# Moving each matmul's activation half to a fixed start in memory

## The chip, the cores and the metric

The kernel runs on one core of one Trainium2 chip. The core has five engines that run side by side: TensorE (PE in the profile) multiplies matrices, VectorE (DVE), ScalarE (ACT) and GpSimd (POOL) work on elements, and SyncE (SP) issues most of the DMA transfers. Operands lie in SBUF, a memory of 128 partitions; TensorE's results go to PSUM. The metric is the device time of one execution in microseconds (us); lower is better.

## What is computed

One step of a one-layer decoder trunk, in float32, for 256 tokens of a new sequence and 8 times 4 tokens of running ones: T = 288 tokens in all, of D = 2048 channels.

```python
h = rmsnorm(x, norm1_g)
proj = h @ w_in + b_in                      # 2048 -> 3072
a, gate, z = split(proj)
u = a * sigmoid(gate)
c = silu(layernorm(depthwise_causal_conv(u_ext, conv_w, conv_b), ln_g, ln_b))
d = multiscale_pool(z_ext, pos0)            # windows 2, 4, 8, 16
p = einsum("btgc,gce->btge", d, pool_w) * pool_scale
x = x + concat([c, p]) @ w_out              # 2048 -> 2048
h2 = rmsnorm(x, norm2_g)
f = square(relu(h2 @ w_ff1))                # 2048 -> 8192
x = x + f @ w_ff2                           # 8192 -> 2048
y = rmsnorm(x, norm_f)
```

The outputs are y and the new states of the convolution and of the pooling.

## The kernel before

Activations lie with channels on the partitions: a tile of 128 channels by 288 tokens. Every product is made of matmuls with a stationary 128x128 block of weights and such a tile as the moving operand, 288 columns wide, adding up in a PSUM bank.

To keep float32 accuracy with TensorE's float32r operands, each operand is split in two halves, a rounded value (hi) and the rest (lo). Activations have tiles like hh and hl (the first norm's output), ah and al (the second's), fh and fl (the squared MLP values), ph and pl, mh and ml (the mixed groups), dh and dl (the pooling). Weights are loaded as raw tiles `wr` of 128 x 4 x 256 words by SP, and split on ScalarE (line 246) and VectorE or GpSimd (line 247) into `whi` and `wlo`. A product of two blocks then takes three matmuls: hi times hi (line 253), weights hi times activation lo (254), weights lo times activation hi (255). `gemm` runs over the activation tiles and, inside, over two output tiles. The first product (lines 316 to 348) does the same in its own loop, with its matmuls on line 342: eight on hh, eight on hl, eight on hh for each pair of activation tiles.

The stages follow one another: the first product and its norm; the other columns of w_in, with the convolution (VectorE, line 395) and the pooling beside them; pool_w; w_out in two halves with the layer norm between; then four times a quarter of w_ff1 (8 groups of 96 matmuls, moving operands ah and al) and a quarter of w_ff2 (8 groups of 96, moving operands fh and fl); and the last norm.

The order of work on each engine is made when the program is built, as are the places of tiles. Pools are laid out one behind the other in the order of the code. The one named `wraw` holds six raw tiles, `wspl` four hi and four lo weight tiles of 4096 bytes a partition. `actp`, right behind it, holds 64 tiles of 288 words, 1152 bytes a partition, end to end: 40 under the tag `act`, 16 under `p`, and 8 under `c`, which hold the convolution's results and later halves of ah and al. Behind it come `tmpp` and `prdp`. A tile is given out in turn, when its last reader is done. Nearly all halves are made by `act` (lines 111 and 112); the convolution's results on line 381.

Of the kernel before, what the change touches and what calls it, by code (L numbers as in the profile page):

```python
# [9 lines left out]
F32 = mybir.dt.float32  # L10
F32R = mybir.dt.float32r
# [5 lines left out]
P = 128  # L17
# [3 lines left out]
T = SEQ + NB * NS  # L21
# [15 lines left out]
ZO = PH + SEQ  # L37
ZL = ZO + NB * ZS
LATER = 1000000


GROUPS = (3, 2, 1, 0)
# [38 lines left out]
def trunk_kernel(ctx: ExitStack, tc: tile.TileContext, io):  # L81
# [6 lines left out]
    actp = ctx.enter_context(tc.tile_pool(name="actp", bufs=40))  # L88
# [8 lines left out]
    def nm(s):  # L97
        seen[s] = seen.get(s, 0) + 1
        return f"{s}{seen[s]}"

    @contextmanager
    def later(by=LATER):

        tc.cur_priority += by
        yield
        tc.cur_priority -= by

    def row(name):
        return rowp.tile([P, T], F32, name=nm(name), tag="row")

    def act(name, **kw):
        return actp.tile([P, T], F32R, name=nm(name), **(kw or {"tag": "act"}))

    def tmp(name, n=T, tag="tmp", bufs=6):
        return tmpp.tile([P, n], F32, name=nm(name), tag=tag, bufs=bufs)
# [1 line left out]
    def ms(name, n=512):  # L117
        return msp.tile([P, n], F32, name=nm(name), tag="ms", padded_shape=[P, 512])
# [10 lines left out]
    def samples(ap, n):  # L129
        return ap.rearrange("p (b t) -> p b t", t=n)  # L130

    def windows(ap, *dims):
        return bass.AP(ap.tensor, ap.offset, [ap.ap[0], *dims])
# [8 lines left out]
    def v(key, j):  # L142
        return vec[:, OFF[key] + j : OFF[key] + j + 1]
# [175 lines left out]
    for c in range(8):  # L319
# [5 lines left out]
        for k0, k1 in steps:  # L325
            for k in range(2 * c + k0, 2 * c + k1):
                hh, hl = act("hh"), act("hl")
                nc.scalar.activation(hh, xT[:, k, :], AF.Copy, scale=v("norm1_g", k))  # L328
                nc.vector.scalar_tensor_tensor(out=hl, in0=xT[:, k, :], scalar=v("norm1_g", k), in1=f32(hh), op0=ALU.mult, op1=ALU.subtract)
                pair.append((hh, hl))  # L330
            if len(steps) == 2:
                r, h, l = [t[:, :, k0, :] for t in views]
            else:
                r, h, l = first_raw[c], hi, lo
            nc.scalar.copy(h, r)  # L335
            nc.vector.tensor_tensor(l, r, h.bitcast(F32) if len(steps) == 2 else f32(hi), op=ALU.subtract)
            for w, x in ((hi, 0), (hi, 1), (lo, 0)):
                if c == 7 and w is lo:
                    token_sum(total, rows[0])
                for k in range(k0, k1):  # L340
                    for m in range(4):
                        nc.tensor.matmul(  # L342
                            first_banks[m][:, :T], lhs(w, k, m), pair[k][x],
                            start=c == 0 and k == 0 and w is hi and x == 0, stop=c == 7 and k == 1 and w is lo,
                        )
                if c == 7 and w is hi and x == 0:
                    square(6)
                    square(7)
                    rows = [row("tot")]
                    nc.vector.tensor_tensor(rows[0], squares[:, 0, 0], squares[:, 0, 1], op=ALU.add)  # L350
# [8 lines left out]
    cs = {}  # L359
# [16 lines left out]
    def conv_taps(pair):  # L376

        with later():
            pc, cw = {}, {}
            for i in pair:  # L380
                cs[i] = actp.tile([P, T], F32, name=nm("c"), tag="c", bufs=8)
                pc[i] = cvp.tile([P, SEQ], F32, name=nm("pc"), tag="cv", padded_shape=[P, 512])
                cw[i] = vec[:, CWO + i * CW : CWO + (i + 1) * CW]
                nc.scalar.activation(pc[i], u_all[:, i, 0:SEQ], AF.Identity, bias=v("conv_b", i), scale=cw[i][:, 0:1])  # L384
            for i in pair:
                prd = prdp.tile([P, NB, NS, CW], F32, name=nm("prd"), tag="prd")
                src = windows(u_all[:, i, UO:UL], (US, NB), (1, NS), (1, CW))
                nc.gpsimd.tensor_tensor(prd, src, cw[i][:, None, None, :].to_broadcast([P, NB, NS, CW]), op=ALU.mult)
                cso = cs[i][:, SEQ:T]
                nc.vector.tensor_reduce(samples(cso, NS), prd, axis=AX.X, op=ALU.add)  # L390
                nc.scalar.activation(cso, cso, AF.Identity, bias=v("conv_b", i))
            for w in range(1, CW):
                for i in pair:
                    dst = pc[i] if w < CW - 1 else cs[i][:, 0:SEQ]
                    nc.vector.scalar_tensor_tensor(out=dst, in0=u_all[:, i, w : w + SEQ], scalar=cw[i][:, w : w + 1], in1=pc[i], op0=ALU.mult, op1=ALU.add)  # L395
            for i in pair:
                if i == 0:
                    nc.gpsimd.tensor_copy(sum_c, cs[i])
                else:
                    nc.gpsimd.tensor_tensor(sum_c, sum_c, cs[i], op=ALU.add)  # L400
# [3 lines left out]
    def pool_group(g):  # L404

        bk = bank2()
        gemm(bk, hx)
        w = WINDOWS[g]
        for m in range(2):
            i = 2 * g + m  # L410
            z = z_all[:, i, :]
            zs = samples(z[:, ZO:ZL], ZS)
            p = bk[m][:, :T]
            nc.vector.tensor_tensor(p, p, rb, op=ALU.mult)
            nc.scalar.activation(z[:, PH:ZO], p[:, 0:SEQ], AF.Identity, bias=v("b_in", 16 + i))
            nc.scalar.activation(zs[:, :, PH:ZS], samples(p[:, SEQ:T], NS), AF.Identity, bias=v("b_in", 16 + i))  # L416
            b = ms("d")[:, :T]
            s, step, n = z, 1, w
            if w > 8:
                s, step, n = tmp("s", ZL, "s", 2), 4, w // 4  # L420
                nc.vector.tensor_reduce(s[:, 3:ZL], windows(z[:, 0 : ZL - 3], (1, ZL - 3), (1, 4)), axis=AX.X, op=ALU.add)
            at = PH - step * (n - 1)
            nc.vector.tensor_reduce(b[:, 0:SEQ], windows(s[:, at:], (1, SEQ), (step, n)), axis=AX.X, op=ALU.add)
            nc.vector.tensor_reduce(samples(b[:, SEQ:T], NS), windows(s[:, ZO + at :], (ZS, NB), (1, NS), (step, n)), axis=AX.X, op=ALU.add)
            nc.vector.tensor_tensor(b[:, 0 : w - 1], b[:, 0 : w - 1], rise[:, g, 0 : w - 1], op=ALU.mult)
            nc.vector.scalar_tensor_tensor(out=b[:, 0:SEQ], in0=b[:, 0:SEQ], scalar=1.0 / w, in1=z[:, PH:ZO], op0=ALU.mult, op1=ALU.subtract)
            bs = samples(b[:, SEQ:T], NS)
            nc.vector.scalar_tensor_tensor(out=bs, in0=bs, scalar=1.0 / w, in1=zs[:, :, PH:], op0=ALU.mult, op1=ALU.subtract)
            dh, dl = act("dh", tag="p", bufs=16), act("dl", tag="p", bufs=16)
            nc.scalar.copy(dh, b)  # L430
            nc.vector.tensor_tensor(dl, b, f32(dh), op=ALU.subtract)
            dd[i] = (dh, dl)
# [3 lines left out]
    def mix_group(g, banks=bank2):  # L436

        bk = banks()
        gemm(bk, [dd[2 * g], dd[2 * g + 1]])
        for m in range(2):  # L440
            i = 2 * g + m
            mh, ml = act("ph"), act("pl")
            nc.scalar.activation(mh, bk[m][:, :T], AF.Copy, scale=v("pool_scale", i))
            nc.vector.scalar_tensor_tensor(out=ml, in0=bk[m][:, :T], scalar=v("pool_scale", i), in1=f32(mh), op0=ALU.mult, op1=ALU.subtract)
            mixp[i] = (mh, ml)
# [7 lines left out]
    conv_gates(1, first_banks[2:4])  # L453
    conv_gates(0, first_banks[0:2])
    conv_taps((0, 1))
    for kind, i in SEQUENCE:
        (conv_group if kind == "conv" else mix_group if kind == "mix" else pool_group)(i)
        if kind == "conv" and (i % 2 or i == 6):
            conv_taps((i,) if i >= 6 else (i - 1, i))
        if i == 3 and kind == "conv":  # L460
            nc.sync.dma_start(z_all[:, :, ZO:ZL], io["hist_p"])
    mix_group(1)
    mix_group(0, lambda: [ms("m") for _ in range(2)])
    with later(2 * LATER):
        nc.sync.dma_start(io["u_out"], u_all[:, :, UO - CH : UL])
# [46 lines left out]
    for g in range(8):  # L512
        bk = bank2()
        gemm(bk, mixc)
        for m in range(2):
# [3 lines left out]
            kw = {"tag": "p", "bufs": 16} if k < 8 else {"tag": "c", "bufs": 8} if k >= 12 else {}  # L519
# [122 lines left out]
```

## Time and profile before

| | us |
|---|---|
| median of 3 runs | 1097.99 (1097.48 to 1098.67) |
| the profiled execution | 1098.09 |
| its span, from the first to the last instruction | 1096.3 |
| TensorE busy | 1082.3 |
| VectorE busy | 631.0 |
| ScalarE busy | 471.8 |
| GpSimd busy | 162.8 |

Busy time counts a stretch once, however many matmuls overlap in it. A matmul's row lasts about 0.3 us from its start to the end of its results, and the next one starts well before that, so the time that a matmul costs is the step from its start to the next start; a window of the trace, divided by the matmuls that it holds, gives that step.

### The profile page before, as it was taken

The page shows a single profiled execution, that of the slowest core. Times are in us where ns is not written, and L with a number is a line of the kernel's source. Part 1 is how long each engine was busy: PE and PEld are TensorE (multiplying, and loading weights), DVE is VectorE, ACT ScalarE, POOL GpSimd, SP SyncE. Part 2 cuts the span into 40 slices and gives each one's busy share as a digit, 9 for nine tenths or more (in the row PEclk, how much of TensorE's full clock was granted, in tenths as well). Part 3 has the DMA queues.
Part 4 walks back from the last instruction along what each step waited for, and adds up shares of the span by engine and source line. Part 5 has one row for each costly group of instructions (what it writes and reads, how often), then busy time and mean ns, then how long its engine had stood idle before and what let it go on. Part 6 is the DMA issues. An engine that isn't in the chain of part 4 may idle for free.

```text
span 1096.3 us, 19737 instructions
## 1 busy us (share of the span) xinstructions
PE 1082.3 (99%) x8186; PEld 1081.0 (99%) x8186; DVE 631.0 (58%) x982; ACT 471.8 (43%) x650; POOL 162.8 (15%) x108
## 2 busy tenths in 40 slices
PE   9999999999999999999999999999999999999995
PEld 9999999999999999999999999999999999999995
DVE  7798989687554544444554444555544445554553
ACT  7544454476444433334443333444433334444441
POOL 0899878500000000000000000000000000000000
PEclk9999999999999999999999999999999999999998
DMA  9655568555555555555555555555555555555522
GB/s 335 221 184 167 173 162 236 161 165 171 158 170 161 170 168 165 168 171 160 170 170 164 167 173 162 167 172 169 161 171 162 166 172 167 162 171 164 166 94 87
DMA packets 56649, 187.04 MB, mean 171 GB/s; under 512 B 5872, under 2 KB 11504, under 8 KB 56560
## 3 DMA queue, kind: packets, MB, share of 16 engines
q1 hardware_dynamic: 56416, 185.74, 54.3%
q8 instruction: 64, 1.05, 0.4%
q14 instruction: 25, 0.20, 0.1%
q10 hardware_dynamic: 144, 0.05, 0.0%
HBM read 181.49 MB, written 4.28 MB: 169 GB/s over the span
## 4 chain that ended last, share of the span: by engine, by line
PE 98%; DVE 1%; ACT 0%; DMA 0%; SPq 0%; issue 0%; DVEq 0%
PE ac L253 32%; PE ac L254 32%; PE ac L255 31%; PE ac L342 1%; PE cv L342 1%; DMA xT<-in_xT 0%; DVE xT L582 0%; PE pr L238 0%; ACT hh L328 0%; ACT uz L312 0%; PE pf L221 0%; ACT whi L335 0%; DVEq L628 0%; PE m L253 0%; PE m L254 0%
## 5 line engine op out<-in xcount | busy, mean ns | idle before, releaser
L246 ACT CAST whi<-wr 128x1024 fp32r<-128x1024 f32 x330 | 346.6, 1051 | 583.9 <-PE ac L254 553.7
L247 DVE TENSOR_TENSOR wlo<-wr,whi 128x1024 fp32r<-128x1024 f32 x272 | 333.3, 1225 | 373.7 <-ACT whi L246 373.7
L253 PE MATMUL ac<-ah,whi 128*128 128x288 f32 x1024 | 303.2, 296 | 0.0
L253 PE MATMUL ac<-fh,whi 128*128 128x288 f32 x1024 | 303.1, 296 | 0.0
L254 PE MATMUL ac<-fl,whi 128*128 128x288 f32 x1024 | 301.7, 295 | 0.0
L254 PE MATMUL ac<-al,whi 128*128 128x288 f32 x1024 | 301.6, 295 | 0.0
L255 PE MATMUL ac<-fh,wlo 128*128 128x288 f32 x1024 | 299.8, 293 | 0.0
L255 PE MATMUL ac<-ah,wlo 128*128 128x288 f32 x1024 | 299.4, 292 | 0.0
L255 PEld LDWEIGHTS ac<-fh,wlo 128*128 128x128 f32 x1024 | 193.5, 189 | 0.0
L255 PEld LDWEIGHTS ac<-ah,wlo 128*128 128x128 f32 x1024 | 193.4, 189 | 0.0
L254 PEld LDWEIGHTS ac<-fl,whi 128*128 128x128 f32 x1024 | 193.0, 188 | 0.0
L254 PEld LDWEIGHTS ac<-al,whi 128*128 128x128 f32 x1024 | 192.6, 188 | 0.0
L253 PEld LDWEIGHTS ac<-ah,whi 128*128 128x128 f32 x1024 | 192.4, 188 | 0.0
L253 PEld LDWEIGHTS ac<-fh,whi 128*128 128x128 f32 x1024 | 192.3, 188 | 0.0
L247 POOL TENSOR_TENSOR wlo<-wr,whi 128x1024 fp32r<-128x1024 f32 x58 | 138.6, 2414 | 25.2 <-ACT whi L246 23.0
L395 DVE SCALAR_TENSOR_TENSOR pc<-uz,vec,pc 128x256 f32<-128x256 f32 x232 | 98.7, 482 | 6.8 <-ACT pc L384 4.8
L253 PE MATMUL ac<-hh,whi 128*128 128x288 f32 x320 | 93.7, 296 | 0.7 <-ACT uz L416 0.7
L254 PE MATMUL ac<-hl,whi 128*128 128x288 f32 x320 | 93.8, 297 | 0.0
L255 PE MATMUL ac<-hh,wlo 128*128 128x288 f32 x320 | 88.5, 295 | 0.0
L253 PEld LDWEIGHTS ac<-hh,whi 128*128 128x128 f32 x320 | 60.3, 188 | 1.0 <-ACT uz L416 1.0
L254 PEld LDWEIGHTS ac<-hl,whi 128*128 128x128 f32 x320 | 60.4, 189 | 0.0
L255 PEld LDWEIGHTS ac<-hh,wlo 128*128 128x128 f32 x320 | 58.5, 189 | 0.0
(153 smaller groups left out, 878.2 us busy)
## 6 DMA issues: line engine op xcount, KB each, us to landing
wr<-in_w SPq DMA_DIRECT2D x336, 512.0 KB, 3.8
out_u_out<-uz SPq DMA_DIRECT2D x1, 1208.0 KB, 9.5
xT<-in_xT SPq DMA_DIRECT2D x2, 576.0 KB, 7.9
out_yT<-xT SPq DMA_DIRECT2D x2, 576.0 KB, 2.9
uz<-in_hist_c SPq DMA_DIRECT2D x1, 1088.0 KB, 11.8
wr<-in_w SPq DMA_DIRECT2D x4, 256.0 KB, 5.1
xT<-in_xT SPq DMA_DIRECT2D x3, 288.0 KB, 5.8
out_z_out<-uz SPq DMA_DIRECT2D x1, 668.0 KB, 9.8
```

The costliest lines, as they stand in the source:

```text
L246: nc.scalar.copy(hi[:, a:b, :], raw[:, a:b, :])
L247: eng.tensor_tensor(lo[:, a:b, :], raw[:, a:b, :], hi[:, a:b, :].bitcast(F32), op=ALU.subtract)
L253: nc.tensor.matmul(b, wh, xh, start=first, stop=False)
L254: nc.tensor.matmul(b, wh, xl, start=False, stop=False)
L255: nc.tensor.matmul(b, wl, xh, start=False, stop=last)
L342: nc.tensor.matmul(first_banks[m][:, :T], lhs(w, k, m), pair[k][x], start=c == 0 and k == 0 and w is hi and x == 0, stop=c == 7 and k == 1 ...
L395: nc.vector.scalar_tensor_tensor(out=dst, in0=u_all[:, i, w : w + SEQ], scalar=cw[i][:, w : w + 1], in1=pc[i], op0=ALU.mult, op1=ALU.add)
```

## The change

Each tile of the pool becomes a slot of 320 words (1280 bytes, five times 256), and the kernel uses 288 words of it from word 23 on. All operations on the halves are the same, on a slice of the slot. The pool grows from 64 x 1152 to 64 x 1280 bytes a partition.

```diff
+SLOT, SHIFT = 320, 23
...
+    def slot(name, dtype, **kw):
+        return actp.tile([P, SLOT], dtype, name=nm(name), **kw)[:, SHIFT : SHIFT + T]
+
     def act(name, **kw):
-        return actp.tile([P, T], F32R, name=nm(name), **(kw or {"tag": "act"}))
+        return slot(name, F32R, **(kw or {"tag": "act"}))
...
-                cs[i] = actp.tile([P, T], F32, name=nm("c"), tag="c", bufs=8)
+                cs[i] = slot("c", F32, tag="c", bufs=8)
```

The first word used then lies 60 bytes past a multiple of 256 in every slot.

## The prediction

> **What bounds the kernel now.** I read the page first (busy shares, the chain that ended last), then TensorE's own waits, then the step from one matmul to the next in each stage.
>
> ```profile
> span 1096.3 us, 19737 instructions
> PE 1082.3 (99%) x8186; PEld 1081.0 (99%) x8186; DVE 631.0 (58%) x982; ACT 471.8 (43%) x650; POOL 162.8 (15%) x108
> ...
> PE 98%; DVE 1%; ACT 0%; DMA 0%; SPq 0%; issue 0%; DVEq 0%
> ```
>
> ```profile
> PE pr L238 <- DVE st L235: 1.3, 1, 1.3
> PE warm L209 <- DVE ones L195: 1.1, 1, 1.1
> PE pf L221 <- ACT q L565: 1.0, 1, 1.0
> PE ac L253 <- ACT uz L416: 0.7, 1, 0.7
> PE ac L342 <- ACT whi L335: 0.4, 1, 0.4
> ```
>
> TensorE (PE) is busy 99% of the span, the chain runs over it for 98%, and all its waits for other engines come to 4.5 us. So the time is the number of matmuls times the step between two of them. The windows by stage (stretch, length, then busy us and count of PE, PEld, DVE, ACT, POOL, then granted clock and DMA) give the step:
>
> ```profile
> 34.00:150.00 116.00, 115.26 (x866) 115.02 (x866) 107.67 (x248) 50.18 (x73) 104.81 (x48) 1.00 0.55 170
> ...
> 290.00:480.00 190.00, 190.00 (x1444) 190.00 (x1443) 91.81 (x105) 72.99 (x90) 0.00 (x0) 1.00 0.54 166
> 480.00:690.00 210.00, 210.00 (x1600) 210.00 (x1600) 101.63 (x115) 80.06 (x99) 0.00 (x0) 1.00 0.55 168
> 690.00:890.00 200.00, 200.00 (x1520) 200.00 (x1520) 96.73 (x111) 77.49 (x96) 0.00 (x0) 1.00 0.54 166
> 890.00:1080.00 190.00, 190.00 (x1448) 190.00 (x1447) 95.99 (x119) 82.74 (x120) 0.00 (x0) 1.00 0.47 147
> ```
>
> In the MLP, 790 us hold 1444 + 1600 + 1520 + 1448 = 6012 matmuls: **131.4 ns each**, at full granted clock. No other engine is near its limit there (DVE 48 to 51%, DMA 47 to 55%). The change touches no matmul's shape and no count; what it can move is this step, through the address that the moving operand is read from.
>
> **Does the step know the address?** SHIFT is 23 words, 92 bytes, and the slots then begin 60 bytes past a multiple of 256; so the pool begins at 60 - 92 = -32, which is 224 past one. Tiles of 1152 bytes (4.5 times 256) end to end therefore begin at 224 and at 96 in turn. The weight tiles lie in the pool just below, in pieces of 4096 bytes, and every stationary block is 512 bytes further on, so every weight load begins at 224. Before, then, each moving half begins either at the weights' own place modulo 256, or 128 bytes from it.
>
> In the first product (L342) hh and hl are taken in turn from an empty pool: all hh begin at 224, all hl at 96. Eight matmuls on hl follow sixteen on hh. Windows laid on such runs, for matmuls that read hl, then for those that read hh:
>
> ```profile
> 17.53:18.60 1.07, 1.07 (x8) 1.00 1.07 392
> 20.71:21.78 1.07, 1.07 (x8) 1.00 1.08 367
> ```
>
> ```profile
> 18.60:20.71 2.11, 2.11 (x16) 1.00 1.05 391
> 21.78:23.88 2.10, 2.10 (x16) 1.00 1.13 356
> ```
>
> At 96: 1.07 / 8 = 133.8 ns. At 224: 2.105 / 16 = 131.6 ns. The operation, shape and weights are the same. In the second MLP product the program's placement turns the pairs over: in its first quarter, from the fifth pair on, fh lies at 224 and fl at 96; in its second quarter fh lies at 96 and fl at 224. One window on each, 72 steps long (the count has 2 more that were still running):
>
> ```profile
> 390.22:399.74 9.52, 9.52 (x74) 1.00 0.51 165
> 592.49:601.93 9.44, 9.44 (x74) 1.00 0.55 167
> ```
>
> 132.2 ns against 131.1 ns. So four arrangements take 131.1, 131.6, 132.2 and 133.8 ns, and the address alone moves the step by up to **2.7 ns**.
>
> How many steps is that worth? The groups of line 253 (out, moving operand, weights, then the count):
>
> ```profile
> L253 PE MATMUL ac<-ah,whi 128*128 128x288 f32 x1024 | 303.2, 296 | 0.0
> L253 PE MATMUL ac<-fh,whi 128*128 128x288 f32 x1024 | 303.1, 296 | 0.0
> L253 PE MATMUL ac<-hh,whi 128*128 128x288 f32 x320 | 93.7, 296 | 0.7 <-ACT uz L416 0.7
> L253 PE MATMUL ac<-ph,whi 128*128 128x288 f32 x128 | 37.7, 296 | 0.0
> L253 PE MATMUL ac<-mh,whi 128*128 128x288 f32 x128 | 35.3, 296 | 0.0
> L342 PE MATMUL ac<-hh,whi 128*128 128x288 f32 x32 | 7.5, 315 | 0.5 <-ACT whi L335 0.4
> L253 PE MATMUL ac<-dh,whi 128*128 128x288 f32 x12 | 3.2, 295 | 0.0
> L253 PE MATMUL m<-dh,whi 128*128 128x288 f32 x4 | 1.2, 296 | 0.0
> ```
>
> Lines 254 and 255 repeat each group of 253: 3 x 2640 = 7920. Line 342 has six such groups of 32 (two targets, three terms): 192. Together **8112 matmuls** read an activation half, so each ns of the step is worth 8.1 us.
>
> Why should it? The timeline shows that the next weights are read while the present operand streams: a load begins in the same 0.01 us as a matmul.
>
> ```profile
> 599.84 0.29 PE L255 MATMUL ac<-fh,wlo 128*128 128x288 f32 x1
> 599.84 0.19 PEld L253 LDWEIGHTS ac<-fh,whi 128*128 128x128 f32 x1
> ...
> 599.97 0.30 PE L253 MATMUL ac<-fh,whi 128*128 128x288 f32 x1
> ```
>
> Two streams of reads start together, and their relative place in memory matters. I read that as the two meeting in some part of SBUF. [...]
>
> **The change, part by part.**
>
> Moving operand at 60 in every matmul. The starts of both streams were equal modulo 128 in every row of before (0 or 128 bytes apart modulo 256); now they are 60 - 224 = -164, that is 92 apart modulo 256, and modulo 64 they are 28 apart. No row shows such a pair, so I bound it. Above: the worst arrangement seen, 133.8, which is also at the start nearest to 60 (36 bytes away): +2.4 ns, +19.5 us. Below: six short matmuls with full weight loads in a row of the chain,
>
> ```profile
> 285.43 0.64 PE pr L238 x6
> ```
>
> 0.64 / 6 = 107 ns for a third of the columns (line 238 streams 96); ours cannot be under that, which allows -24 ns, or -198 us: far, and no likely end. I take one full width of the effect that the rows show, downwards: 131.4 - 2.7 = 128.7 ns. The reason for the sign is that all known arrangements have the two streams in step modulo 128, the case in which they meet most, and the change is the first to take them out of it. The size is a choice, an estimate from the spread of the rows. 8112 x 2.7 ns = **-21.9 us**.
>
> Writers of the slots. The same instructions write and read them:
>
> ```profile
> L548 ACT CAST fh<-f 128x288 fp32r<-128x288 f32 x64 | 24.2, 425 | 0.0
> L549 DVE TENSOR_TENSOR fl<-f,fh 128x288 fp32r<-128x288 f32 x64 | 26.3, 452 | 0.6 <-ACT fh L548 0.6
> L559 DVE TENSOR_TENSOR xT<-xT,ac 128x288 f32<-128x288 f32 x64 | 27.3, 455 | 26.9 <-PE ac L255 26.9
> L328 ACT ACTIVATE hh<-xT,vec 128x288 fp32r<-128x288 f32 x16 | 8.4, 530 | 2.5 <-DMA xT<-in_xT 1.7 <-DMA vec<-in_vec 0.8
> ```
>
> fl, between slots at 224 and 96, takes 452 ns and an operation of the same shape outside the pool (L559) 455, so these two engines show no care for the place. Were a start at 60 to cost them 10%, it would be 45 to 53 ns each. Cover: DVE and ACT are half idle in the MLP. On the chain only three hh lie, while TensorE waits for its first operands (start, us, what):
>
> ```profile
> 6.41 0.54 ACT hh L328
> ...
> 8.03 0.44 ACT hh L328
> ...
> 9.04 0.43 ACT hh L328
> ```
>
> I cost it at 0, between -0.1 and +1.4 us (each of the three a tenth shorter, or twice as long).
>
> Conv tiles c, pool tiles dh and dl. The same argument; DVE is the one engine near its limit, 107.67 of 116 us in the convolution stretch. If TensorE gains there and DVE doesn't, its 866 matmuls keep their time and 866 x 2.7 = 2.3 us of the gain are lost. I leave the gain in: PE has 115.26 of these 116 us and waits for DVE nowhere in it.
>
> Room. 64 slots are 128 bytes longer, 8192 bytes in all; tiles behind the pool move up by 32 times 256 and keep their phase. No instruction, DMA or wait is added, no buffer count changes, no queue is passed. When PE steps 2% faster, weights have to come 2% faster: DMA at 55% and the splits on ACT and DVE at half cover that; nothing is late next. The tail after the last matmul reads xT, which doesn't move.
>
> **Sum.** The profiled execution took 1098.1 us, 1.8 over its span; the median of the runs is 1098.0, so both stand for one another. 1098.1 - 21.9 + 0 = **1076.2 us**.
>
> **The rivals.**
>
> *The meeting goes away wholly.* Then the step loses well over one width: at two to three widths, 123 to 126 ns, 44 to 66 us, 1032 to 1054. For it: the best seen arrangement is only 2.7 below the worst, so all four may be bad ones. Against: nothing shows such a step lasting. [...]
>
> *Slower: the start's own place sets the step, and 60 behaves as its neighbour 96.* Runs with the operand at 96 alone take 133.8 ns, more than any mixture; the change makes every matmul such a run. 8112 x 2.4 = +19.5: 1117.6. For it: 36 bytes is the smallest distance to any known start. Against: mixtures in which two of three matmuls read at 96 are the fastest of all (131.1). It decides as soon as the MLP's step is above 131.7.
>
> *Slower: a start inside a unit of reading costs one unit more.* All starts before are multiples of 32; 60 is none. If the unit is 16 bytes, a half has 72 units from an aligned start and 73 from 60: 131.4 / 72 = 1.8 ns, +14.8 us, 1113. No row can show it or exclude it. Were the unit 64 bytes, 32 and 60 past it touch 19 units alike, at no cost. [...]
>
> *The change does nothing to be seen.* If only bit 7 of the address counts and mixtures average out, all-60 steps 131.4 +- 0.2 ns: 1096 to 1100.
>
> **How the numbers follow.** Forecast (1058 to 1092) 0.42; wholly gone (1032 to 1058) 0.18; neighbour 96 (1105 to 1120) 0.16; one unit more (1100 to 1115) 0.14; nothing 0.10. Faster 0.60, same 0.10, slower 0.30, with 0.2% of 1098, 2.2 us, as what a measurement can tell from no change. The range leaves out half of the wholly-gone case and the upper half of the neighbour case: 1044 to 1114. Both signs hold much of the chance; the likeliest one's own range is 1058 to 1092.
>
> **What would show it.** Right: the same 8186 matmuls; the four stretches of the MLP hold about 2% more matmuls for their length, 128.7 ns each; the runs on hh and hl in the first product, and both kinds of window in the second MLP product, become equal, since all halves now begin alike. Wrong: unequal runs (then it isn't the moving start), a step over 131.7 (a slower rival; 133.2 points to one unit more, 133.8 to the neighbour), longer L548 or L549 rows, PE waits of more than 5 us in all, or a gain only in stages that DVE leaves alone.

## The result and the profile after

| | before | after |
|---|---|---|
| median of 4 runs, us | 1097.99 | 1082.97 (1082.41 to 1083.48) |
| ratio | | 0.9863, 95% interval 0.9846 to 0.988 |
| profiled span, us | 1096.3 | 1081.2 |

The change makes the kernel 15.0 us faster, against 21.9 forecast. First the head of the page after and its chain by engine, then all of TensorE's waits:

```profile
span 1081.2 us, 19737 instructions
PE 1066.8 (99%) x8186; PEld 1065.2 (99%) x8186; DVE 630.5 (58%) x982; ACT 470.7 (44%) x650; POOL 162.6 (15%) x108
...
PE 98%; DVE 1%; ACT 0%; DMA 0%; SPq 0%; DVEq 0%; issue 0%
```

```profile
PE pr L242 <- DVE st L239: 1.3, 1, 1.3
PE warm L213 <- DVE ones L199: 1.1, 1, 1.1
PE pf L225 <- ACT q L569: 1.0, 1, 1.0
PE ac L346 <- ACT whi L339: 0.8, 1, 0.8
PE ac L257 <- ACT uz L420: 0.8, 1, 0.8
```

The same 19737 instructions, the same 8186 matmuls, the same chain. TensorE's waits are 5.0 us where they were 4.5. So nothing was moved or added, and no new wait took the place of the time that went; every matmul merely costs less. Where that happened can be read from points that both chains pass: the start of the short matmuls behind each norm, and of the last sum. Before, then after (start, us, what):

```profile
33.06 0.64 PE pr L238 x6
...
217.68 0.64 PE pr L238 x6
...
1080.36 0.43 PE pf L221 x6
```

```profile
32.42 0.64 PE pr L242 x6
...
213.09 0.64 PE pr L242 x6
...
279.80 0.64 PE pr L242 x6
1065.15 0.43 PE pf L225 x6
```

With the row at 285.43 that the prediction shows, the stretches are 33.06, 184.62, 67.75, 794.93 and 15.94 us before, and 32.42, 180.67, 66.71, 785.35 and 16.05 after. They lose 0.6, 4.0, 1.0 and 9.6 us and gain 0.1. The tail, which reads xT, is untouched; every stage that streams activation halves lost time. (Of the first 0.6, the first x tile's earlier landing is 0.5: the first hh starts at 5.95 us after, 6.41 before.)

The windows show what became of the step. In the first product, on matmuls that read hl, then hh; then two stretches of the second MLP product, in the quarters that held the two mixtures before, 72 steps each (the count again has 2 that were still running):

```profile
17.16:18.20 1.04, 1.03 (x8) 1.00 1.06 399
20.29:21.32 1.03, 1.03 (x8) 1.00 1.06 381
```

```profile
18.20:20.29 2.09, 2.08 (x16) 1.00 1.05 391
21.32:23.41 2.09, 2.08 (x16) 1.00 1.12 357
```

```profile
388.00:397.36 9.36, 9.36 (x74) 1.00 0.58 175
592.49:601.85 9.36, 9.36 (x74) 1.00 0.52 170
```

8 steps in 1.03 to 1.04 us, 16 in 2.09, 72 in 9.36: 130 ns everywhere, within the 0.01 us to which a window is laid. The differences between hl and hh (133.8 and 131.6) and between the two quarters (132.2 and 131.1) are gone. From start to start, over all 8112 matmuls on halves but for some thirty steps across a wait or a change of stage, the mean step fell from 131.86 to 130.00 ns, and 1.86 x 8080 steps are 15.0 us: the whole result.

The engines that write the slots did not notice:

```profile
L333 DVE SCALAR_TENSOR_TENSOR hl<-xT,vec,hh 128x288 fp32r<-128x288 f32 x16 | 8.2, 518 | 4.0 <-ACT hh L332 4.0
L552 ACT CAST fh<-f 128x288 fp32r<-128x288 f32 x64 | 24.1, 423 | 0.0
L553 DVE TENSOR_TENSOR fl<-f,fh 128x288 fp32r<-128x288 f32 x64 | 26.4, 452 | 0.6 <-ACT fh L552 0.6
```

fl takes 452 ns as before, fh 423 against 425, hl 518 against 513.

### The profile page after: what moved, and what is told of

It reads as the page before. It is cut to its first block, busy times and chain, and to the rows that moved or that the text cites. A ratio compares the mean times of both kernels' runs of the same rounds, so it can differ in the third digit from the quotient of the medians.

```text
span 1081.2 us, 19737 instructions
## 1 busy us (share of the span) xinstructions
PE 1066.8 (99%) x8186; PEld 1065.2 (99%) x8186; DVE 630.5 (58%) x982; ACT 470.7 (44%) x650; POOL 162.6 (15%) x108
## 4 chain that ended last, share of the span: by engine, by line
PE 98%; DVE 1%; ACT 0%; DMA 0%; SPq 0%; DVEq 0%; issue 0%
PE ac L257 32%; PE ac L258 32%; PE ac L259 32%; PE ac L346 1%; PE cv L346 1%; DVE xT L586 0%; DMA xT<-in_xT 0%; PE pr L242 0%; ACT hh L332 0%; ACT uz L316 0%; PE pf L225 0%; ACT whi L339 0%; DVEq L632 0%; PE m L259 0%; PE m L258 0%
## 5 line engine op out<-in xcount | busy, mean ns | idle before, releaser
L257 PE MATMUL ac<-ah,whi 128*128 128x288 f32 x1024 | 298.7, 292 | 0.0
L257 PE MATMUL ac<-fh,whi 128*128 128x288 f32 x1024 | 298.6, 292 | 0.0
L258 PE MATMUL ac<-al,whi 128*128 128x288 f32 x1024 | 298.5, 292 | 0.0
L258 PE MATMUL ac<-fl,whi 128*128 128x288 f32 x1024 | 298.5, 291 | 0.0
```

Of the source, the lines that this page charges most:

```text
L257: nc.tensor.matmul(b, wh, xh, start=first, stop=False)
L258: nc.tensor.matmul(b, wh, xl, start=False, stop=False)
```

## The experiments

In all of them but w1, w2 and n1, which say so, only places change. The times are of one execution each, beside the kernel before at 1097.6 to 1098.2 us; the step is what counts, and it is the mean from start to start of matmuls whose neighbours begin alike, over hundreds of matmuls. Theory A is the prediction's reason: what counts is the distance between the starts of the moving operand and of the weight load.

**One start for all: at the weights' place (word 0 of the slot), and 128 from it (word 32).**

```diff
-SLOT, SHIFT = 320, 23
+SLOT, SHIFT = 320, 0
```

> The slots stay and every activation half begins 224 past a multiple of 256 (word 0 of its slot), which is the place of the weight loads too. Theory A (the step is set by where the moving operand's start lies against the start of the weight load; in step is bad): 131.6 ns a matmul, as in the runs on hh of before, so about 1097 us, no better than before. Theory B (it is enough that all starts are alike; mixing two starts is what cost time): 130.0 ns as with 60, about 1083 us.

> Every half begins 96 past a multiple of 256 (word 32 of its slot), 128 bytes from the place of the weight loads. Theory A, with the runs on hl of before as its row: 133.4 to 133.8 ns a matmul, about 1110 to 1114 us, slower than before. Theory B: 130.0 ns, about 1083 us.

Windows in w_ff1 and in the second MLP product, of e1, then of e2:

```profile
295.00:355.00 60.00, 60.00 (x458) 1.00 0.53 167
390.00:460.00 70.00, 70.00 (x534) 1.00 0.53 167
```

```profile
295.00:355.00 60.00, 60.00 (x452) 1.00 0.51 163
390.00:460.00 70.00, 70.00 (x527) 1.00 0.52 164
```

The changed kernel has 464 and 541 in the same windows. From start to start: 131.67 ns at 224 and 1096.1 us; 133.33 ns at 96 and 1109.8 us. So theory B falls: making all starts alike is worth 2 us with 224 and costs 12 with 96. The slots as such bring nothing; word 23 does.

**A map of starts.** Each stage gets one start of its own, so that one run measures eight. Theory F, in the last of the texts, takes 130.0 ns as the floor of the step.

```diff
-    def slot(name, dtype, **kw):
-        return actp.tile([P, SLOT], dtype, name=nm(name), **kw)[:, SHIFT : SHIFT + T]
+    def slot(name, dtype, at=SHIFT, **kw):
+        return actp.tile([P, SLOT], dtype, name=nm(name), **kw)[:, at : at + T]
...
-                fh, fl = act("fh"), act("fl")
+                fh, fl = act("fh", AT_F[ch]), act("fl", AT_F[ch])
```

> One start for each stage: w_in product 240, pooling and mixed p 0, mixed c 16, w_ff1 32, the four quarters of w_ff2 48, 64, 80 and 88 past a multiple of 256. Theory A: the steps differ from stage to stage by ns, with the worst near 224 and 96 and the best near 60. Theory B: 130.0 ns in every stage. Theory C (a start inside a 16-byte line costs or saves something of its own): the starts that are multiples of 16 have one step, and 60 another.

> One start for each stage, close to 60: w_in product 28, pooling and mixed p 36, mixed c 40, w_ff1 44, the quarters of w_ff2 52, 56, 68 and 72 past a multiple of 256. Theory A: steps that change smoothly or by one level around the 130.0 ns at 60. Theory B: 130.0 ns everywhere. Theory C: 60 stands out among its neighbours, since it leaves one word in its first 64 bytes (or its first 16).

> One start a stage, weights at 224: w_in 236, pooling and mixed p 252, mixed c 12, w_ff1 16, the quarters of w_ff2 76, 92, 24 and 8. If 60 is good because it is 12 past a multiple of 16, then 236, 252, 12, 76 and 92 take about 130 ns too; if every start has its own step, they spread over 130 to 137 as the earlier ones did. 16 is to be near 130.3 again, now over 3000 matmuls.

> 128 bytes are put between the weight tiles and the pool, to reach the other half of the 256 bytes; weights stay at 224. One start a stage: w_in 220, pooling and mixed p 204, mixed c 172, w_ff1 188, the quarters of w_ff2 108, 124, 140 and 156, all 12 past a multiple of 16. Theory A: 188 is 128 from 60 and lies as far out of step modulo 128, so about 130.0; the others between 130 and 134. If the whole 256 bytes count, 188 has a step of its own, as 224 and 96 have (131.7 and 133.3).

> Starts in the other half of the 256 bytes, as in s4, at multiples of 16: w_in 112, pooling and mixed p 128, mixed c 144, w_ff1 160, the quarters of w_ff2 176, 192, 208, and 200 (8 past one). Theory F with 130.0 as the floor: none is under 130.0; the multiples of 16 lie between 130 and 135, and 200 over 131. A step under 130.0 would be a start better than 60.

The starts are those of the texts above. One window of 70 us in the first quarter of w_ff2 of s2 (start 52), and one in its second quarter (56):

```profile
390.00:460.00 70.00, 70.00 (x515) 1.00 0.50 161
590.00:660.00 70.00, 70.00 (x527) 1.00 0.52 165
```

515 and 527 matmuls where the changed kernel, at 60, has 541 in each. All the steps, each a mean over its stage, by the start's bytes past a multiple of 16 (the start itself modulo 256, then ns):

| past 16 | starts and steps |
|---|---|
| 0 | 0: 133.3; 16: 130.3 (mixed c), 132.5 (w_ff1); 32: 132.0; 48: 131.1; 64: 131.7; 80: 134.7; 96: 133.3; 112: 130.9; 128: 133.3; 144: 131.4; 160: 133.3; 176: 133.3; 192: 133.3; 208: 132.0; 224: 131.7; 240: 131.7 |
| 4 | 36: 135.0; 52: 136.7; 68: 136.7 |
| 8 | 8: 135.5; 24: 134.7; 40: 133.4; 56: 133.3; 72: 133.3; 88: 136.3; 200: 136.7 |
| 12 | 12: 130.0; 28: 133.3; 44: 131.7 (130.0 and 133.3, see below); 60: 130.0; 76: 133.3; 92: 133.3; 108: 133.3; 124: 130.0; 140: 130.0; 156: 130.0; 172: 130.0; 188: 131.1; 204: 133.3; 220: 130.0; 236: 131.2; 252: 130.0 |

Three things follow. The step knows the address to 4 bytes: 56, 60 and 64 take 133.3, 130.0 and 131.7. No start is under 130.0; eight take it throughout, all of them 12 past a multiple of 16; of the three starts measured that are 4 past one, none is under 135.0. And the change could as well have gone the other way: most starts measured are no better than the 131.9 of before. Theory B falls again. Of theory C the half holds that the place inside 16 bytes matters, but a start inside is as often the best as the worst, and what would make 16 bytes a line no run shows. Theory A's claim that the effect is worst in step falls as well: 52 and 68, 84 and 100 bytes from the weights, are worse than 224 and 96. Nor does the place modulo 128 decide alone, as 188, 128 bytes from 60, takes 131.1.

One start does not always give one step. In s2, w_ff1 has the start 44 in all four quarters. A window of 60 us in each:

```profile
295.00:355.00 60.00, 60.00 (x464) 1.00 0.54 172
490.00:550.00 60.00, 60.00 (x452) 1.00 0.52 167
695.00:755.00 60.00, 60.00 (x452) 1.00 0.52 167
900.00:960.00 60.00, 60.00 (x464) 1.00 0.53 172
```

Less the two that were still running at the start of each, that is 130.0 ns in the first and fourth quarter and 133.3 in the second and third, with the same start, shape and operation in one run. 16 takes 132.5 ns in w_ff1 of s3; in the mixed c of s1 it takes 132.5 up to a single step of 163 ns, and 130.0 from there on. 32 (131.7 and 132.2) and 112 (131.1 and 130.2) have two steps as well. In these rows of matmuls single steps repeat in a pattern: 131 and 129 ns in turn at 60, 132, 138, 137 and 140 (each within 1 ns) at 52. A start thus allows one such pattern or a few, and where the pattern changed, it changed between stages or behind an interruption. What chooses it is not known. 60 took 130.0 ns in every stage of the changed kernel; most other starts were measured in one stage or quarter only.

**Moving the weights instead.** A tile of 32 bytes ahead of the weight pool moves every weight load from 224 to 0, and the starts of the stages are chosen anew (all modulo 256).

```diff
+    gap = ctx.enter_context(tc.tile_pool(name="gap", bufs=1)).tile([P, 8], F32, name="gap")
     wspl = ctx.enter_context(tc.tile_pool(name="wspl", bufs=4))
```

> 32 bytes are put ahead of the weight tiles, so that every weight load begins at 0 instead of 224 past a multiple of 256, and the moving halves take one start a stage. Theory A (only the distance from the weights' start counts): w_ff1 at 92 has the distance of 60 before, 130.0 ns; mixed c at 32 that of 0, 133.3; the quarters of w_ff2 at 60, 0, 84, 52 those of 28, 224, 52, 20: 133.3, 131.7, 136.7 and unknown. Theory C (the moving operand's own address counts, the weights' doesn't): w_in and the first quarter of w_ff2 at 60 take 130.0, mixed c at 32 131.9, the second quarter at 0 133.3, the fourth at 52 136.7.

Windows in w_in (60), w_ff1 (92) and the first, second and third quarter of w_ff2 (60, 0, 84):

```profile
60.00:130.00 70.00, 70.00 (x528) 1.00 0.55 173
```

```profile
295.00:355.00 60.00, 60.00 (x463) 1.00 0.56 169
390.00:460.00 70.00, 70.00 (x527) 1.00 0.54 163
590.00:660.00 70.00, 70.00 (x534) 1.00 0.53 166
795.00:865.00 70.00, 70.00 (x515) 1.00 0.54 159
```

92 is now the fast one with 130.0 ns, and 60 takes 133.3 in both stages that have it; 32 takes 133.4, 0 takes 131.7 and 84 takes 136.7. Each is the step that the start at the same distance from the weights had while these lay at 224. Theory C misses at 60, 32 and 0, by 3.3, 1.5 and 1.6 ns; only its 136.7 at 52 is met (136.6, in the fourth quarter), where theory A had no value. That much of theory A is shown: **the distance from the weight load's start counts, the address by itself does not.**

**Is it weight reads that meet moving reads?** Then shorter loads should help, and by theory A the step should fall with the columns.

```diff
-    def product(bank, rhs, w, first, last):
+    def product(bank, rhs, w, first, last, n=P):
...
+        n = P if first or last else n
-        (xh, xl), (wh, wl), b = rhs, w, bank[:, :T]
+        (xh, xl), (wh, wl), b = rhs, [t[:, :n] for t in w], bank[:n, :T]
...
-                gemm(bk, fx)
+                gemm(bk, fx, cols=(32, 64, 96, 128)[ch])
```

> The changed kernel, all halves at 60, but in the quarters of w_ff2 all matmuls except those on the first and the last activation pair load only 32, 64, 96 and 128 weight columns and give that many rows of the output; the product is left incomplete by that. [...]

> As w1, with the moving halves of w_ff2 at 52 past a multiple of 256, where the step with full loads is 136.7 ns, and 32, 64, 96 and 128 weight columns in its quarters (but for the first and last pair; the product is incomplete). Theory A in its narrow form (the part of the step above 130 comes from weight reads that meet moving reads, the 130 itself does not): the step falls with the columns from 136.7 to 130.0 at 32 columns. Theory G (what counts is only where the two reads begin): 136.7 in all four quarters.

The loads of w1 did become shorter, 107 ns at 32 columns against 187 at 128:

```profile
L258 PEld LDWEIGHTS ac<-fh,whi 128*128 128x128 f32 x352 | 65.9, 187 | 0.2
...
L258 PEld LDWEIGHTS ac<-fh,whi 128*32 128x32 f32 x224 | 24.1, 107 | 4.9
```

Yet the windows in its four quarters (32, 64, 96, 128 columns) hold what the changed kernel holds (541, 541, 541, 464), or two more:

```profile
390.00:460.00 70.00, 70.00 (x541) 1.00 0.55 172
590.00:660.00 70.00, 70.00 (x543) 1.00 0.54 172
795.00:865.00 70.00, 70.00 (x541) 1.00 0.56 170
1000.00:1060.00 60.00, 60.00 (x464) 1.00 0.37 115
```

130.0, 129.3, 130.0 and 130.0 ns, 1081.7 us in all. With a quarter of the weight reads the step is the same (at 64 columns it is 0.7 ns less), so theory A's picture of two streams that disturb each other all along is wrong at this start. At 52, the windows of w2 in the first (32 columns) and the last quarter (128):

```profile
390.00:460.00 70.00, 70.00 (x520) 1.00 0.51 163
1000.00:1060.00 60.00, 60.00 (x442) 1.00 0.48 155
```

Between two loads of one length the step is 135.0, 135.0, 135.6 and 136.7 ns: of the 6.7 above 130.0, the length of the load accounts for 1.7, and the narrow form, which had 130.0 at 32 columns, falls. Theory G, which had 136.7 in all four, comes closest: where the two reads begin sets most of it.

**What is the 130.0 made of?**

```diff
+        n = T if first or last else n
-        (xh, xl), (wh, wl), b = rhs, w, bank[:, :T]
+        (xh, xl), (wh, wl), b = [t[:, :n] for t in rhs], w, bank[:, :n]
...
-                gemm(bk, fx)
+                gemm(bk, fx, cols=(240, 256, 272, 288)[ch])
```

> The changed kernel with all halves at 60; in the quarters of w_ff2 the matmuls (but for those on the first and last pair) stream only 240, 256, 272 and 288 of the 288 tokens, which leaves the product of the other tokens incomplete. [...]

The windows in its four quarters:

```profile
375.00:445.00 70.00, 70.00 (x616) 1.00 0.61 194
565.00:635.00 70.00, 70.00 (x585) 1.00 0.57 183
760.00:830.00 70.00, 70.00 (x559) 1.00 0.54 175
960.00:1020.00 60.00, 60.00 (x463) 1.00 0.52 167
```

Between two short matmuls the step is 111.7, 118.9 and 125.0 ns, and 130.0 at 288 columns. It goes with the length: 48 columns less take 18.3 ns off, and nothing holds it at 130.0. From one length to the next, 16 columns apart, it grows by 7.2, 6.1 and 5.0 ns. The shorter operands end at other places, which may be why these three differ; that was not separated. Whether a fixed cost between matmuls is part of the 130.0, as theory F has it, the four lengths do not show.

**A mixture that beats both?**

```diff
+AT = dict(hh=11, hl=23, dh=23, dl=23, ph=23, pl=7, mh=7, ml=11, ah=23, al=11)
+AT_F = ((11, 23), (23, 7), (32, 23), (12, 23))
```

> Before, the mixture of hi at 96 and lo at 224 took 131.1 ns, less than 133.3 and 131.7 with either start alone. So each stage now has one start for its hi halves and another for its lo halves: w_in 12 and 60, mixed p 60 and 252, mixed c 252 and 12, w_ff1 60 and 12, the quarters of w_ff2 12 and 60, 60 and 252, 96 and 60, 16 and 60. Theory F (130.0 is streaming and a fixed cost between matmuls, the floor): none under 130.0, the pairs of 12, 60 and 252 at it. Theory K (what counts is each passage from one start to the next, and mixing can beat both): some pair under 130.0, which would be a version faster than the changed kernel.

Windows in w_ff1 (hi at 60, lo at 12) and the second quarter of w_ff2 (60 and 252):

```profile
295.00:355.00 60.00, 60.00 (x463) 1.00 0.55 170
590.00:660.00 70.00, 70.00 (x537) 1.00 0.53 166
```

12 with 60 takes 130.0 ns in all three places that have it. 60 with 252 takes 131.1 and 252 with 12 takes 131.0, though each of the three starts alone takes 130.0; 96 with 60 takes 132.2, which is just the mean of 133.3 for two matmuls of three and 130.0 for the third, and 16 with 60 takes 131.1. None is under 130.0, 1087.3 us in all. So what two starts take in turn does not follow from each alone, as theory K has it, but the gain that it held possible did not come. No version tried that does the whole work is faster than the changed kernel.

## Why the prediction came out as it did

- **The bound** held: time is the number of matmuls times the step. Some 8080 steps shorter by 1.86 ns are 15.0 us, the whole difference.
- **Its starting value was a little low.** It divided 790 us by 6012, but each window counts two matmuls that still ran at its start; without these eight it is 131.6 ns in the MLP, and 131.9 over all stages.
- **That the address moves the step**, and that all pairs of windows become equal, held: 130.0 ns in each.
- **The term that was mis-sized** is the one chosen as an estimate, one full width of the effect, -2.7 ns and -21.9 us. It measured -1.86 ns and -15.0 us. The prediction took a step of 128.7 to be in reach; 130.0 is the least of 42 starts.
- **The reason for the sign** held in part. The place of one start relative to the other counts (r1), as it said. That distances in step modulo 128 are the worst, and any other better, did not hold: 224 and 96 take 131.7 and 133.3, and out-of-step 52, 68 and 200 take 136.7. And a quarter of the weight reads left the step at 130.0 ns (w1), which speaks against two streams that meet all along; that they meet at all, in some part of SBUF, is the author's reading and was not shown. Outside the one place 60, the same argument would have forecast a gain for starts that cost up to 5 ns a matmul. So the sign came out right by luck in the start, not by the rule.
- **The edits costed at nothing** cost nothing to be seen: fl 452 ns, fh 423, no new wait. The convolution stretch, where VectorE might have kept the gain back, lost 4.0 us between the first two norms, more than its share.
- **The rivals.** The neighbour: 96 alone does take 133.3 ns (e2), but 60 does not behave like it, since 4 bytes already make a difference of 3.3 ns. One unit more: 60 crosses one more 16-byte boundary than a start at a multiple of 16, yet none of those is better; no run shows a unit of reading of 16 bytes, nor the 1.8 ns that one more was to cost. The meeting wholly gone: it had 123 to 126 ns, and none of the 42 starts took less than 130.0. Nothing: it had only bit 7 of the address count, but 60 and 96, in which that bit is the same, take 130.0 and 133.3 ns. Nor does the moving address count alone: with the moving start at 60, moving the weights took the step from 130.0 to 133.3 ns (r1).

What stays open is the mechanism: why the distance of the starts counts to 4 bytes, while the length of the weight load hardly does (0.7 ns at most at 60, 1.7 ns at 52). Start and end of the moving operand move together in these runs, except in n1, so which of them it is was not separated. Nor is it known what decides between the two steps that each of 16, 32, 44 and 112 took, nor whether places beyond 256 bytes play a part.

## What to carry to other kernels

When a kernel is a long row of matmuls without waits, divide a stretch by its count and compare the step between tiles at different places: here such a difference was worth 15.0 us, with TensorE 99% busy before and after. If the addresses matter, give each stage another offset and read eight of them from one run; then take the best one through every stage, since a start can have more than one step (44 took 130.0 and 133.3 ns). Choose the offset by what was measured, relative to the weights (60 took 130.0 ns, and 133.3 with the weights moved by 32 bytes), and measure again when anything ahead of either pool changes its size.

## What the runs showed of the hardware

- The mean step of a float32r matmul of 288 columns on a 128x128 block, with all moving operands of a stage at one start modulo 256, lay between 130.0 and 136.7 ns at full granted clock (1.00 in the windows). It goes with the moving operand's start relative to the weight load's, and 4 bytes change it (133.3, 130.0 and 131.7 at 56, 60 and 64). Many steps fall on levels 1.7 ns apart: 130.0, 131.7, 133.3, 135.0, 136.7.
- The start does not fix the step fully: 44 took 130.0 ns in two quarters of w_ff1 and 133.3 in the other two, in one run.
- Moving the weights by 32 bytes moved the steps by 32 bytes at all five distances that were measured before and after (130.0 at 92 in place of 60).
- A weight load's own time goes by 27 ns for 32 columns (107, 133, 160 and 187 ns at 32, 64, 96 and 128), while the step at 60 stays at 130.0 ns (129.3 at 64 columns).
- Two starts that each take 130.0 ns (60 and 252) take 131.1 when they take turns as hi and lo.
